# Up-projection block products: the order of modulation steps, one more PSUM bank, and an operand kept without its shift

## The chip, the cores and the metric

One core of a Trainium2 chip runs the whole program. The metric is the device time of one execution in microseconds (us). The kernel before took 2954.84 us (median of three runs, 2954.62 to 2957.98).

## The reference

A backbone of two layers over 1024 latent tokens and 256 context tokens, width 1024. Each layer has a token mixer and a ConvFFN, and each of the two reads its input through a modulated RMSNorm whose shift and scale come from conditioning vectors:

```python
ml = (silu(c) @ w_mod[i] + b_mod[i]).reshape(B, N_MOD, 1, D)    # six vectors for the latents
mc = (silu(c_ctx) @ w_mod[i] + b_mod[i]).reshape(N_MOD, D)      # six for the context
def modulate(x, shift, scale): return rms_norm(x) * (1.0 + scale) + shift
def conv_ffn(h, w_up, conv_w, conv_b, w_down):
    g, u = split(h @ w_up)                       # 2 x 2816 columns
    acc = conv_b + sum(shifted(g, j) * conv_w[j] for j in range(3))
    return (silu(acc) * u) @ w_down
```

The case is about `h @ w_up` in both layers. The context goes through layer 0's ConvFFN only.

## The kernel before

All tensors are held transposed: 128 channels on the partitions, tokens along the free dimension, in chunks 0 and 1 (512 latents each) and, in layer 0, chunk 2 (256 context tokens). A float32 product is made of three matmuls on a high and a low part of each operand (`mm3`, L72), so each operand is split: the high part is a rounded copy (ACT or POOL), the low part a subtraction (DVE).

**The up-projection** (class `Up`, L1615) makes 22 pairs f of a gate column block and an upper column block, each 128 wide. The first two, f = 0 and 1, are plain products (`plain`). From f = 2 on, gate and upper of both latent chunks are computed together as one 2x2 block product with seven products in place of eight (`PROD`): operands are sums of weight blocks (`s1` to `s4`, made by POOL, split by ACT and DVE) and sums of token blocks (`t1` to `t4`, class `Parts`, made once in the head). The products add up in three PSUM banks per f: x (products 1, 2), y (6, 7, 4) and z (5, 3). Between two products of one bank an engine reads the intermediate sum: `s1` (ACT, L1974) reads x between 1 and 2, `u2` (DVE, L1978) reads y between 6 and 7, `u3` (L1984) reads y after 7, `c22` (L1987) reads z between 5 and 3, `c11`, `c12` and `c21` finish gate and upper. In layer 0 the context's two plain products per f stand between them (`context`).

**Order of the work.** The order on PE, DVE, ACT and POOL is written out by hand in `head` (L1747: f = 0, 1, the token sums, and products 1 and 2 of f = 2) and `turn(f)` (L1848: products 6, 5, 7 of f, product 1 of the next f, product 3 of f, product 2 of the next, product 4 of f). SP, which issues the DMAs, is not in that hand-written order: its order is the planner's. In a turn ACT, DVE and POOL also do the short convolution (`conv`, `conv2`), silu and the product with the upper half (`mix`) of the f whose gate is finished; `store` writes the result row to DRAM. For f = 0 that stands in the head, for f = 1 in turn 2, ahead of `u2`. The result rows (`su`) are two buffers used in turn.

**Modulation vectors.** Layer 0's turns also make the modulation columns that come later. One step (`Up.mod`, L1739) takes one entry of `mods1` (53 are left when the turns start), loads 128x1024 weights into the single buffer `wm` (L1743) and reduces them on DVE (L325) against the conditioning vector: twice, for latents and context, in the first 21 entries, once in the other 32. For the scales (`n in (1, 4)`) a small POOL addition (L330) follows. A turn calls it three times: after `u2`, after product 7 (both ahead of `u3` and `c22` on DVE), and at the end.

**The operand.** For the ConvFFN's input `modulate_kept` (L255) overwrites the residual tile with the modulated operand, because the token sums need it: DVE or POOL scales it in place, ACT writes the high part and, for the operands that DVE scaled, in a second pass adds the shift in place (L272), DVE subtracts (L277).

**Weights.** The raw up-projection weights go through two buffers `raw` (L1633); f = 1's two blocks are split in the head, `raw[1,0]` at its start and `raw[1,1]` behind the chunk-1 gate product of f = 0.

Of the kernel before, what the change touches and what calls it, by code (L numbers as in the profile page):

```python
# [44 lines left out]
def backbone(tc, a):  # L45
# [209 lines left out]
    def modulate_kept(k, x, r, m, first, dst, pool=True):  # L255
# [6 lines left out]
        def scale():  # L262
            if even:
                V.scalar_tensor_tensor(out=x, in0=x, scalar=sc, in1=r, op0=ALU.mult, op1=ALU.mult)
            else:
                P.tensor_mul(x, x, r)
                P.tensor_scalar(out=x, in0=x, scalar1=sc, scalar2=sh, op0=ALU.mult, op1=ALU.add)
# [1323 lines left out]
    class Parts:  # L1591


        def __init__(self, up, j):
            self.up, self.j = up, j
            (self.b11, self.b12), (self.b21, self.b22) = [[xl[k][:, half_of(c)] for c in (0, 1)] for k in (j, j + 4)]
# [7 lines left out]
        def high(self, t, pair):  # L1604
            self.up.B[t, self.j] = pair
            S.copy(pair[0], self.src(t))
# [4 lines left out]
        def low(self, t):  # L1611
            hi, lo = self.up.B[t, self.j]
            V.tensor_sub(lo, self.src(t), f32(hi))

    class Up:  # L1615
# [3 lines left out]
        def __init__(self, l, sp, pairs, mods=()):  # L1619
# [3 lines left out]
            self.mods = list(mods)  # L1623
            self.raw, self.sums, self.A, self.B, self.bank, self.fs, self.spare = {}, {}, {}, {}, {}, {}, {}
            self.d_act = tc.dram_tile([NF, 128, T], F32, name=f"d_act{l}")
# [6 lines left out]
        def load(self, f, s):  # L1632
            self.raw[f, s] = wpool.tile([128, 1024], F32, name="raw", tag="raw", bufs=2)  # L1633
# [86 lines left out]
        def product(self, f, i):  # L1720
            w, b, z = self.PROD[i]
            first = i in (1, 6, 5)
# [16 lines left out]
        def mod(self, n=1):  # L1739
            for _ in range(n):  # L1740
                if self.mods:
                    j = self.mods.pop(0)
                    wm = self.sp.tile([128, D], F32, name="wm", tag="wm", bufs=1)  # L1743
                    mod_cols(*j, mod_load(*j[:3], wm), junk=self.tile("junk").bitcast(BF16))


        def head(self, w, b00, n1):  # L1747


            f0, f1 = F(self, 0), F(self, 1)  # L1750
            self.fs = {0: f0, 1: f1}
            ctx = 2 in self.chunks
# [3 lines left out]
            w1 = [self.halves(0)]  # L1756
            self.split_halves(self.raw[1, 0], w1[0])()
            self.load(2, 0)
# [12 lines left out]
            w1.append(self.halves(1))  # L1771
            self.split_halves(self.raw[1, 1], w1[1])()
            self.load(2, 1)
# [22 lines left out]
            t = [self.sp.tile([128, 1024], F32, name="wm", tag="wm", bufs=1)]  # L1796
            f0.temps = [t[0][:, :512], t[0][:, 512:]]
            for c in (0, 1):
                f0.conv(c)
                f0.conv2(c)  # L1800
                f0.silu(c)
            for c in (0, 1):
                f0.mix(c, V)
            if ctx:
                f0.conv(2)
                f0.conv2(2)
                f0.silu(2)
                f0.mix(2, V)
            f0.store()
# [11 lines left out]
            self.fs[2].s1()  # L1821
# [11 lines left out]
            self.product(2, 2)  # L1833
            self.fs[2].c11()
# [11 lines left out]
            self.spare["t"] = [x[6][:, 512:], x[7][:, :512], x[7][:, 512:]]  # L1846

        def turn(self, f):  # L1848
# [5 lines left out]
            if f == 2:  # L1854
                for c in (0, 1):
                    old.conv(c)
                    old.conv2(c)
                    old.silu(c)
            else:
# [7 lines left out]
            old.mix(1)  # L1867
            old.mix(0)
            if f == 2 and ctx:
                old.conv(2)  # L1870
                old.conv2(2)
                old.silu(2)
                old.mix(2)
            old.store()
# [10 lines left out]
            self.mod()  # L1885
# [7 lines left out]
            self.mod()  # L1893
# [6 lines left out]
            me.c22()  # L1900
            if not n:
# [41 lines left out]
    class F:  # L1943


        def __init__(self, up, f):
            self.up, self.f = up, f
            self.cw = [convw[:, up.l, i, f : f + 1] for i in range(4)]
            self.su, self.t, self.temps = row(1, name="su"), {}, None
# [4 lines left out]
        def open(self):  # L1954
            self.g = row(0, name="g")
# [24 lines left out]
        def c11(self):  # L1980
            S.copy(self.g_of(0), self.bank("x"))
# [28 lines left out]
        def mix(self, c, eng=P, u=None):  # L2010
            eng.tensor_mul(self.s_of(c), self.t[c], self.s_of(c) if u is None else u)  # L2011

# [111 lines left out]
    mods1 = [(0, 5, k, (0, 1)) for k in range(8)] + [(1, n, k, (0, 1) if n < 2 else (0,)) for n in range(6) for k in range(8)]  # L2124
    up = Up(0, sp, [("hi", "lo"), ("x", "y"), ("x", "y"), ("x", "z")], mods1)
# [79 lines left out]
    for i, *fs in (  # L2205
# [10 lines left out]
        if i > 12:  # L2216
            w0[i - 13] = wload(a["wup"][0, i - 13])
    o.product(15)
# [627 lines left out]
    for i in range(10, 15):  # L2846
        o.product(i)
        window(i, (n0, 2 * i - 20) if i < 14 else None, n1.add if i < 14 else last, lambda: up.spill(i - 9, 1))
        if i > 12:
            w0[i - 13] = wload(a["wup"][1, i - 13])  # L2850
    o.product(15)
# [7 lines left out]
    n1.split()  # L2859
    up.plain(w0[0], 0, range(6, 8), b00)  # L2860
    n1.total()
    w0[1] = w0[1]()
    up.load(1, 1)
    n1.root()
# [305 lines left out]
```

## Time and profile before

| | |
|---|---|
| median of the runs | 2954.84 us |
| profiled execution | 2955.65 us |
| its span (first to last instruction) | 2953.7 us |
| mean granted TensorE clock | 0.985 |
| PE matmul, PE weight load, DVE, ACT, POOL busy | 95, 79, 74, 43, 36% of the span |

PE is TensorE's matmul, DVE VectorE, ACT ScalarE, POOL GpSimd, SP the engine that issues DMAs ("SPq" its queue). Times in rows are us from the span's start. A granted clock of 1.00 is the upper level of TensorE's clock (2.4 GHz), 0.50 the lower (1.2 GHz). A row of the timeline gives start, duration, engine, line, operation, tiles (written <- read), shapes, and in brackets how long the engine stood before it and who released it.

Layer 0's up-projection takes from about 698 to 1342 us: turn 2 starts at 776.70 and turn 21, the last, at 1318.21. Layer 1's turn 2 starts at 2289.79, its turn 3 at 2317.75 and its turn 21 at 2668.63.

### The profile page before, as it was taken

Reading aid. Unit: us, or ns where it says so; the run is one execution under the profiler, and the core shown is the slowest. Engines: PE = TensorE matmul, PEld = TensorE weight load, DVE = VectorE, ACT = ScalarE, POOL = GpSimd, SP = SyncE. Lnnn points to the kernel's source line nnn. Section 1 sums busy time; section 2 is a strip of 40 time slices with the busy share of each in tenths; the row PEclk is TensorE's granted clock in tenths of the full one; section 3 lists DMA queues with packets and bytes.
Section 4 is the critical chain, followed back from the end, with each engine's and each line's share of the span. In section 5 each row is a group of like instructions: output and inputs, shape, how many; then the busy total and the mean of one; then the engine's idle time right before and its main releaser. Section 6 shows DMA issues by size and latency. Waiting matters only on the chain.

```text
span 2953.7 us, 40163 instructions
## 1 busy us (share of the span) xinstructions
PE 2798.1 (95%) x14654; PEld 2321.0 (79%) x14654; DVE 2179.0 (74%) x3639; ACT 1257.5 (43%) x2546; POOL 1062.0 (36%) x1069
## 2 busy tenths in 40 slices
PE   7988999999788999999999998999998999999997
PEld 3857888887677788788888777999876788887886
DVE  5688888777776766668776878888756556568766
ACT  5525888725422232332101444888744333333104
POOL 2142444752234444431101534444331444442112
PEclk9999999999899999999999999999999999999998
DMA  6144001372133333345221110000041222226311
GB/s 224 69 147 128 23 15 57 119 249 85 66 103 113 111 119 128 128 139 196 74 70 52 43 36 29 1 1 1 19 142 55 71 80 82 83 86 231 97 58 57
DMA packets 97229, 264.89 MB, mean 90 GB/s; under 512 B 11908, under 2 KB 21060, under 8 KB 96904
## 3 DMA queue, kind: packets, MB, share of 16 engines
q1 hardware_dynamic: 97032, 262.33, 26.6%
q8 instruction: 115, 1.88, 0.3%
q14 instruction: 82, 0.67, 0.1%
HBM read 212.53 MB, written 49.75 MB: 89 GB/s over the span
## 4 chain that ended last, share of the span: by engine, by line
PE 54%; DVE 10%; issue 4%; DMA 4%; ACT 3%; POOL 2%; DVEq 0%; ACTq 0%; POOLq 0%
PE d L72 18%; PE y L72 7%; PE x L72 6%; PE z L72 6%; PE p L72 4%; DMA wm<-in_wmod 3%; PE pv L1281 3%; PE b L72 3%; PE T L1268 2%; PE S L1201 1%; PE qk L72 1%; PE S L1203 1%; PE S L1202 1%; DVE x L325 1%; DVE wm L325 1%
## 5 line engine op out<-in xcount | busy, mean ns | idle before, releaser
L2072 DVE SCALAR_TENSOR_TENSOR x<-d,mod,x 128x512 f32<-128x512 f32 (+1 forms) x352 | 254.9, 734 | 95.9 <-PE d L72 94.7
L1250 POOL TENSOR_SCALAR p<-p,sm 128x1280 f32<-128x1280 f32 x128 | 171.2, 1338 | 288.3 <-DVE sm L1249 190.7
L1271 DVE TENSOR_TENSOR tl<-T,th 128x512 fp32r<-128x512 f32 x328 | 225.5, 687 | 46.8 <-ACT th L1270 42.0
L1281 PE MATMUL pv<-th,v 128*128 128x256 f32 x976 | 254.1, 309 | 1.4 <-ACT vo L1410 1.0
L1224 DVE TENSOR_REDUCE mx<-S 128x1 f32<-128x512 f32 (+1 forms) x400 | 233.8, 585 | 11.0 <-PE S L1203 3.8
L72 PE MATMUL d<-act,wh 128*128 128x512 f32 (+1 forms) x832 | 231.4, 364 | 0.0
L1270 ACT CAST th<-T 128x512 fp32r<-128x512 f32 x328 | 192.2, 586 | 84.2 <-PE T L1268 76.5
L2055 ACT CAST act<-act 128x512 fp32r<-128x512 f32 (+1 forms) x110 | 61.5, 577 | 385.5 <-PE d L72 230.5
L2011 POOL TENSOR_TENSOR su<-x,su 128x512 f32<-128x512 f32 (+1 forms) x83 | 132.3, 1598 | 255.9 <-ACT x L2008 167.2
L72 PE MATMUL x<-h,a1h 128*128 128x512 f32 x640 | 205.3, 402 | 18.0 <-ACT su L1974 15.6
L72 PE MATMUL b<-h,wh 128*128 128x512 f32 (+1 forms) x752 | 206.7, 362 | 5.7 <-DVE h L493 4.0
L1974 ACT COPY su<-x 128x512 f32<-128x512 f32 x40 | 23.5, 587 | 420.9 <-PE x L72 395.4
L1684 POOL TENSOR_TENSOR x<-raw 128x512 f32<-128x512 f32 x80 | 112.8, 1410 | 228.6 <-DMA raw<-in_wup 125.7
L1268 PE MATMUL T<-ident,p 128*128 128x128 f32 x1280 | 193.0, 272 | 1.5 <-POOL p L1250 1.5
L1268 PEld LDWEIGHTS T<-ident,p 128*128 128x128 f32 x1280 | 156.5, 140 | 34.9 <-POOL p L1250 3.2
L1281 PE MATMUL pv<-tl,v 128*128 128x256 f32 x656 | 177.4, 282 | 0.0
L1281 PEld LDWEIGHTS pv<-th,v 128*128 128x128 f32 x976 | 173.4, 189 | 2.4 <-ACT vo L1410 1.5
L72 PEld LDWEIGHTS d<-act,wh 128*128 128x128 f32 x832 | 149.0, 188 | 27.3
L72 PEld LDWEIGHTS b<-h,wh 128*128 128x128 f32 x752 | 133.1, 189 | 35.2 <-DVE h L493 5.4
L72 PEld LDWEIGHTS x<-h,a1h 128*128 128x128 f32 x640 | 122.9, 193 | 48.1 <-ACT su L1974 16.2
L72 PE MATMUL d<-act,wl 128*128 128x512 f32 (+1 forms) x416 | 151.5, 364 | 0.0
L325 DVE CUSTOM_DVE_ANT_0 wm<-wm,silc,bmod 128x1024 f32<-128x1024 f32 x72 | 108.6, 1508 | 53.0 <-DMA wm<-in_wmod 51.6
(501 smaller groups left out, 8188.7 us busy)
## 6 DMA issues: line engine op xcount, KB each, us to landing
raw<-in_wup SPq DMA_DIRECT2D x88, 512.0 KB, 3.4
wm<-in_wmod SPq DMA_DIRECT2D x72, 512.0 KB, 3.7
act<-d_act SPq DMA_DIRECT2D x88, 256.0 KB, 3.6
raw<-in_wdn SPq DMA_DIRECT2D x44, 512.0 KB, 4.3
raw<-in_wout SPq DMA_DIRECT2D x32, 512.0 KB, 3.4
d_act<-su SPq DMA_DIRECT2D x22, 640.0 KB, 3.5
d_act<-su SPq DMA_DIRECT2D x22, 512.0 KB, 2.8
raw<-in_win SPq DMA_DIRECT2D x20, 512.0 KB, 3.6
```

The lines of the kernel that those rows point to most:

```text
L72: PE.matmul(out, w, x, start=first and i == 0, stop=last and i == n - 1, skip_group_check=more)
L325: V.tensor_tensor_reduce(out=out, in0=wm, in1=silc[w], op0=ALU.mult, op1=ALU.add, scale=1.0, scalar=bmod[:, l, i : i + 1], accum_out=mod[l ...
L1224: V.reduce_max(mx[:, j : j + 1], s, axis=AX.X)
L1250: P.tensor_scalar(out=self.p, in0=self.p, scalar1=sm[:, 3:4], scalar2=1.0, op0=ALU.mult, op1=ALU.mult)
L1268: PE.transpose(tb[:, (2 * j + i) * 128 : (2 * j + i) * 128 + 128], rows[i].p[:, c : c + 128], ident)
L1270: S.copy(hi, tb)
L1271: V.tensor_sub(lo, tb, f32(hi))
L1281: PE.matmul(out[0], st, mv, start=(u + j == 0 and x == 0), stop=(u + j == n - 1 and x == len(ops) - 1))
L1684: eng.tensor_tensor(out=t, in0=self.src(f, x), in1=self.src(f, y), op=op)
L2011: eng.tensor_mul(self.s_of(c), self.t[c], self.s_of(c) if u is None else u)
L2055: S.copy(hi, f32(lo))
L2072: V.scalar_tensor_tensor(out=x, in0=b, scalar=mod[self.l, c // 2][:, 40 + d : 41 + d], in1=x, op0=ALU.mult, op1=ALU.add)
```

## The change

- `modulate_kept` no longer adds the shift to the kept tile. ACT makes the high part with the shift as bias, DVE the low part as (x + shift) - high. `Parts` adds the shift where a token sum needs it (t2: the shift of the lower block, t3: the difference `gap`, a new 128x4 tile).
- In the head, product 2 of f = 2 gets a bank "w" of its own. `s1` of f = 2 moves to the end of the head; `c11` of f = 2 becomes a DVE addition of bank w and the copied row, and moves into turn 2.
- The split of f = 1's weights (`second`) stands ahead of the head: `raw[1,1]` is loaded earlier, into the buffer `wm`, and split ahead of w0[1]'s low part; `raw[1,0]` is split behind `n1.root()`.
- Convolution, silu, mix and store of f = 0 and f = 1 become `rest()`: f = 1's stands behind `u2` in turn 2 (it stood ahead of it), f = 0's stays in the head in layer 0 and moves behind `u2` of turn 3 in layer 1, where f = 0 has rows of its own.
- `Up.mod` reduces the weights that the step before loaded, and then loads the next into the same single buffer. The second step of a turn moves behind `u3` and `c22`. Turn 2 has no first step. The entries of `mods1` are reordered: doubled and single ones alternate until the doubled ones are used up.

```diff
         def high():
-            if even:
-                S.activation(hi, x, AF.Identity, bias=sh)
-                S.activation(x, x, AF.Identity, bias=sh)
-            else:
-                S.copy(hi, x)
+            S.activation(hi, x, AF.Identity, bias=sh)
         def low():
-            V.tensor_sub(lo, x, f32(hi))
+            V.scalar_tensor_tensor(out=lo, in0=x, scalar=sh, in1=f32(hi), op0=ALU.add, op1=ALU.subtract)
...
-        def mod(self, n=1):
-            for _ in range(n):
-                if self.mods:
-                    j = self.mods.pop(0)
-                    wm = self.sp.tile([128, D], F32, name="wm", tag="wm", bufs=1)
-                    mod_cols(*j, mod_load(*j[:3], wm), junk=self.tile("junk").bitcast(BF16))
+        def mod(self):
+            if self.wm:
+                mod_cols(*self.wm.pop(), junk=self.tile("junk").bitcast(BF16))
+            if self.mods:
+                j = self.mods.pop(0)
+                self.wm.append((*j, mod_load(*j[:3], self.sp.tile([128, D], F32, name="wm", tag="wm", bufs=1))))
+        def second(self, s):
+            self.w1[s] = self.halves(s)
+            self.split_halves(self.raw[1, s], self.w1[s])()
+            self.load(2, s)
...
-            self.fs[2].s1()
             f1.upper(1, self.plain(w1[1], 1))
...
-            self.product(2, 2)
-            self.fs[2].c11()
+            self.product(2, 2, "w")
...
+            self.fs[2].s1()
+            self.mod()
...
             self.product(f, 6)
-            if f == 2:
-                for c in (0, 1):
-                    old.conv(c)
-                    old.conv2(c)
-                    old.silu(c)
-            else:
+            if f > 2:
                 old.c21()
...
             me.u2()
-            self.mod()
+            if f == 2:
+                old.rest()
+                me.c11(True)
+            else:
+                if f == 3 and not ctx:
+                    self.fs[0].rest()
+                self.mod()
...
-            self.mod()
             if n:
                 for s in ("s1", "s2", "s3"):
                     self.sum(n, s)
...
             me.u3()
             me.c22()
+            self.mod()
...
+    dbl, sgl = [[j for j in mods1[3:] if len(j[3]) == n] for n in (2, 1)]
+    mods1 = mods1[:3] + [x for p in zip(dbl, sgl) for x in p] + sgl[len(dbl) :]
...
+    up.load(1, 1)
     o.product(15)
...
     mod2(3)
+    up.second(1)
     up.plain(w0[0], 0, range(6, 8), b00)
     n1.total()
     w0[1] = w0[1]()
-    up.load(1, 1)
     n1.root()
+    up.second(0)
     up.head(w0, b00, n1)
```

## Rows read from the trace of the kernel before

**Rows 1.** The page, busy us, share of the span and instructions of each engine.
```profile
PE 2798.1 (95%) x14654; PEld 2321.0 (79%) x14654; DVE 2179.0 (74%) x3639; ACT 1257.5 (43%) x2546; POOL 1062.0 (36%) x1069
```

**Rows 2.** Stretches of layer 0: us, busy by engine, clock, DMA share, GB/s.
```profile
771.42:776.70 5.28, 5.28 (x12) 4.12 (x13) 3.70 (x6) 3.81 (x8) 0.00 (x0) 0.50 0.29 105
776.70:816.35 39.65, 29.02 (x134) 23.97 (x132) 25.96 (x34) 14.33 (x26) 13.55 (x13) 0.86 0.22 70
816.35:1026.82 210.47, 186.52 (x926) 153.13 (x924) 149.50 (x207) 57.94 (x98) 83.85 (x93) 0.98 0.33 110
1026.82:1292.97 266.15, 256.53 (x1322) 215.19 (x1320) 174.62 (x241) 83.15 (x140) 109.24 (x118) 1.00 0.37 122
1292.97:1318.21 25.24, 25.24 (x134) 21.53 (x133) 13.31 (x19) 8.28 (x14) 10.09 (x11) 1.00 0.41 141
```

**Rows 3.** The same view for layer 1: turn 2, and turns 3 to 20.
```profile
2289.79:2317.75 27.96, 22.00 (x86) 17.39 (x85) 15.74 (x21) 11.69 (x20) 9.80 (x10) 0.88 0.16 57
2317.75:2668.63 350.88, 350.88 (x1514) 284.22 (x1513) 211.99 (x270) 116.66 (x199) 171.22 (x163) 1.00 0.25 86
```

**Rows 4.** PE's waits in layer 0's turns 2 to 20: total us, times, longest.
```profile
PE z L72 <- DVE su L1987: 18.1, 14, 2.6
PE y L72 <- DVE x L1978: 12.6, 7, 8.3
PE x L72 <- DVE a1l L1673: 8.6, 10, 1.5
PE x L72 <- POOL a1h L1668: 2.4, 2, 1.2
```

**Rows 5.** PE's waits in layer 0's head, 698 to 776.7 us.
```profile
PE x L72 <- ACT su L1974: 6.3, 1, 6.3
PE p L72 <- DVE wl L111: 2.6, 2, 2.0
```

**Rows 6.** PE's waits in layer 1's head and turn 2, 2228 to 2318 us.
```profile
PE x L72 <- ACT su L1974: 9.2, 1, 9.2
PE y L72 <- DVE x L1978: 6.0, 1, 6.0
PE p L72 <- DVE h L277: 3.3, 5, 1.0
```

**Rows 7.** Timeline of ACT at the end of layer 0's head.
```profile
770.78 0.58 ACT L1974 COPY su<-x 128x512 f32<-128x512 f32 x1 [2.43 <-DMA d_act<-su]
```

**Rows 8.** Timeline of DVE in layer 0's turn 2: convolution, then u2.
```profile
780.49 0.74 DVE L2004 SCALAR_TENSOR_TENSOR x<-g,convw,x 128x512 f32<-128x512 f32 x1
...
788.60 0.48 DVE L2005 SCALAR_TENSOR_TENSOR x<-g,convw,x 128x256 f32<-128x256 f32 x1
...
790.14 0.68 DVE L1978 TENSOR_TENSOR x<-y,su 128x512 f32<-128x512 f32 x1
```

**Rows 9.** Timeline of SP's queue in layer 0's turn 3.
```profile
819.57 0.33 SPq L311 DMA_DIRECT2D wm<-in_wmod  x1
822.46 0.33 SPq L2014 DMA_DIRECT2D d_act<-su  x1
```

**Rows 10.** Timeline of DVE in layer 0's turn 3.
```profile
819.46 0.69 DVE L1993 TENSOR_TENSOR su<-y,su 128x512 f32<-128x512 f32 x1
...
823.09 1.42 DVE L325 CUSTOM_DVE_ANT_0 x<-wm,silc,bmod 128x1024 bf16<-128x1024 f32 x1 [1.21 <-DMA wm<-in_wmod]
...
825.77 1.22 DVE L1673 TENSOR_TENSOR a1l<-raw,a1h 128x1024 fp32r<-128x1024 f32 x1
830.04 2.27 DVE L325 CUSTOM_DVE_ANT_0 x<-wm,silc,bmod 128x1024 bf16<-128x1024 f32 x1 [3.05 <-DMA wm<-in_wmod]
...
834.29 0.69 DVE L1987 TENSOR_TENSOR su<-z,su 128x512 f32<-128x512 f32 x1
```

**Rows 11.** Timeline of DVE and POOL in layer 0's head, token sums.
```profile
752.53 1.67 POOL L1684 TENSOR_TENSOR x<-raw 128x512 f32<-128x512 f32 x1 [52.42 <-DVE t L1613]
753.08 1.67 DVE L1600 TENSOR_TENSOR x<-x 128x512 f32<-128x512 f32 x1
```

More of the change, by code (lines that the diff above doesn't have):

```diff
@@ L1605, in high @@
             self.up.B[t, self.j] = pair
-            S.copy(pair[0], self.src(t))
+            if t in self.shift:
+                S.activation(pair[0], self.src(t), AF.Identity, bias=self.shift[t])
+            else:
+                S.copy(pair[0], self.src(t))
         def src(self, t):
@@ L1612, in low @@
             hi, lo = self.up.B[t, self.j]
-            V.tensor_sub(lo, self.src(t), f32(hi))
+            if t in self.shift:
+                V.scalar_tensor_tensor(out=lo, in0=self.src(t), scalar=self.shift[t], in1=f32(hi), op0=ALU.add, op1=ALU.subtract)
+            else:
+                V.tensor_sub(lo, self.src(t), f32(hi))
     class Up:
@@ L1718, in operand, with product @@
             return H[c][j + 4 * k]
-        def product(self, f, i):
+        def product(self, f, i, own=None):
             w, b, z = self.PROD[i]
-            first = i in (1, 6, 5)
+            first = i in (1, 6, 5) or own is not None
+            z = own or z
             if first:
@@ L1795, in head @@
                 p.low(1)
[L1796 to L1809 removed]
+            if ctx:
+                t = self.sp.tile([128, 1024], F32, name="wm", tag="wm", bufs=1)
+                f0.temps = [t[:, :512], t[:, 512:]]
+                f0.rest()
             f1.gate(1, self.plain(w1[0], 1))
@@ L1866, in turn @@
                     down.act_load(e)
[L1867 to L1874, printed above, removed]
+            if f > 2:
+                old.mix(1)
+                old.mix(0)
+                old.store()
             self.alow(f, 1)
@@ L1978, in u2, with c11 @@
             V.tensor_add(self.u, self.bank("y"), self.s_of(0))
-        def c11(self):
-            S.copy(self.g_of(0), self.bank("x"))
+        def c11(self, apart=False):
+            if apart:
+                V.tensor_add(self.g_of(0), self.bank("w"), self.s_of(0))
+            else:
+                S.copy(self.g_of(0), self.bank("x"))
         def u3(self):
@@ L2011, in mix, with rest @@
             eng.tensor_mul(self.s_of(c), self.t[c], self.s_of(c) if u is None else u)
+        def rest(self):
+            for c in (0, 1):
+                self.conv(c)
+                self.conv2(c)
+            for c in (0, 1):
+                self.silu(c)
+                self.mix(c, V)
+            if 2 in self.up.chunks:
+                self.conv(2)
+                self.conv2(2)
+                self.silu(2)
+                self.mix(2, V)
+            self.store()
         def store(self):
@@ L2850, in backbone @@
             w0[i - 13] = wload(a["wup"][1, i - 13])
+    up.load(1, 1)
     o.product(15)
@@ L2859, in backbone @@
     n1.split()
+    up.second(1)
     up.plain(w0[0], 0, range(6, 8), b00)
@@ L2862, in backbone @@
     w0[1] = w0[1]()
-    up.load(1, 1)
     n1.root()
+    up.second(0)
     up.head(w0, b00, n1)
```

32 lines of the change are left out of this document (17 added, 15 removed).

## The prediction

> **What bounds the kernel now.** The page's busy times come first [rows 1]: TensorE (PE) is busy for 95% of the span and the next engine, VectorE (DVE), for 74%. So a change pays only where PE stands still, or where the granted clock is down. The stretches of the two up-projections come next. In layer 0 the five stretches of [rows 2] run from the end of the head to the last turn: turn 20, with no gap at all, takes 25.24 us, which is the floor of a layer-0 turn; turn 2 takes 39.65, turns 3 to 9 take 210.47 (30.07 each), turns 10 to 19 take 266.15 (26.6 each). In layer 1 [rows 3] turns 3 to 20 take 350.88, or 19.49 each, and PE is busy for all of it: nothing is to be won there. Seven products in 19.49 make 2.79 us a product. Turn 2 of layer 1 takes 27.96.
>
> So 61.9 us over the floor lie in layer 0's turns 2 to 20 (14.4 in turn 2, 47.5 after it), 8.5 in layer 1's turn 2, and some in the heads. The list of waits says who ended PE's gaps. In layer 0's turns [rows 4]: 18.1 us for `c22` (L1987), which must read bank z before product 3 adds to it; 12.6 for `u2` (L1978), 8.3 of it at once in turn 2; 8.6 for a1's low part; 2.4 for its high part on POOL. In layer 0's head [rows 5]: 6.3 for the copy `s1` (L1974), which must read bank x before product 2 adds to it, and 2.6 for a low part (L111). In layer 1 up to turn 2 [rows 6]: 9.2 for `s1`, 6.0 for `u2`, 3.3 for the low parts of the modulated operand (L277). A gap also brings the clock down: after layer 0's 6.3 us gap twelve matmuls took 5.28 us at a granted 0.50, the lower of the two levels [rows 2], where 2.79 is the product at the upper one: 2.5 us.
>
> **The change part by part.** The sum is made against the profiled execution, 2955.65 us (span 2953.7), which is 0.8 above the median 2954.84.
>
> **Own bank for the head's second product.** Product 2 no longer adds to bank x, so it doesn't wait for `s1`. Layer 0: the gap of 6.3, its refill (0.3) and the 2.5 at half clock go, 9.1 together. Layer 1: 9.2, 0.3 and 2.1 go, 11.6. The price is `c11` as a DVE addition out of PSUM instead of an ACT copy, 0.69 us like L1987 [rows 10], in turn 2. Also `s1` moves behind the last splits, so ACT no longer stands for the store of f0's row there, 2.43 us [rows 7].
>
> **f1's weights split early.** The split of `raw[1,1]` now stands ahead of w0[1]'s low part on DVE: two more 128x512 subtractions of 0.69. In layer 0 PE already waits for that low part (part of the 2.6 in [rows 5]): +1.3, and I add 1.0 for a lower clock behind the longer gap (bounds 0 and the 2.5 seen). In layer 1 PE shows no wait there, and I cost it at nothing: earlier PE work covers it, and without the cover it is the same 1.3.
>
> **Shift out of the operand.** One ACT pass per operand goes; the low part becomes a three-operand DVE op of the kind that takes 0.74 us [rows 8] against 0.69. This can give back at most the 3.3 of [rows 6], at least 0; I take 3.0, since DVE then has only two ops per operand and ACT one. Layer 0 shows no such wait, so nothing. The later operands with a bias add under 0.1 us each and lie beside PE work.
>
> **f1's convolution behind `u2`.** In turn 2, DVE did the convolution [rows 8], a2's low part and then `u2` at 790.14, while PE stood 8.3. Now `u2` comes first. `u2` ended at 790.8; without the chain of 8.5 us ahead of it (780.49 to 789.0) and with ACT 2.9 earlier (the 2.43 and a copy) it ends near 779.4. PE starts turn 2 6.8 earlier (the head's sum, below), at 769.9, and reaches product 7 two products later, at 775.5: a wait of 3.9 stays (bounds 0 and the old 8.3). What is queued behind the moved work is a1's low part, and product 1 of the next f waits for that: four ops of 0.75, two mixes of 0.69, the third chunk's three of 0.5, `c11` 0.69 and about 1 us for ACT's silu, then 1.22 for the low part [rows 8, 10]: 8.5 us after `u2`, where PE wants it 3.3 after (one product and two matmuls). So a new wait of 5.2. Bounds: 0, if it fills DVE's idle time, and 9. With 0.6 of refill and 1.5 of clock, turn 2 becomes 25.24+3.9+5.2+2.1 = 36.4: it gives 3.2. Layer 1 lacks the third chunk, so 6.5 stand in place of 8.5 and 3.2 in place of 5.2; f0's convolution has left its head too, so ACT and DVE come sooner and I take 2.0 for the wait at product 7, between 0 and 3.9: 19.49+2.0+3.2+1.5 = 26.2, which gives 1.8; f0's convolution, moved to turn 3 behind `u2`, costs 1.0 there in the same way (bounds 0 and 3).
>
> In the heads, then: layer 0 gives 9.1-2.3 = 6.8, layer 1 11.6+3.0 = 14.6.
>
> One row speaks against the moved convolution: a DVE subtraction of two SBUF tiles took 1.67 us beside a POOL addition [rows 11], where ops of its size take 0.69 [rows 10]. POOL's a1 high part now falls beside the moved convolution. The Trainium skill (SBUF — State Buffer, "Who interferes with whom") has it that a DVE op with both inputs in SBUF contends with GpSimd's reads; by that rule each turn 2 would be about 1 us longer, and the total about 2 us more than mine, by the row's difference. I leave it inside the range.
>
> **Modulation weights.** The load one step ahead gives nothing by itself: the buffer is single, and the load is already issued at 819.57 [rows 9], where the last reduction ends and `c21` starts [rows 10]. What pays is the place of the second step. Today DVE waits 3.05 us for its load until 830.04, reduces twice, and only then runs `u3` and, at 834.29, `c22` [rows 10]; now `u3` and `c22` stand ahead of it, and the 18.1 us for `c22` go. The first step stays between `u2` and a1's low part. There the alternation of double and single reductions helps: a pair of steps (last of one turn, first of the next) has three reductions instead of four, 1.3 less (half of the 2.68 from 823.09 to 825.77), against waits of 1.5 for a1's low part. I keep 0.6 per turn in turns 3 to 10. In turns 11 to 16 a doubled scale (n=1) or an n=4 puts its POOL addition ahead of a1's high part, the 2.4 us of [rows 4]: 2.2 per turn. Turns 17 to 20: 0.3. With 3.0 for clock: 4.8+13.2+1.2+3.0 = 22.2 of the 47.5 remain, and 25.3 go. Bounds: all 47.5, or 11 (rival 2).
>
> **Sum:** 6.8+3.2+25.3 in layer 0, 14.6+1.8-1.0 in layer 1: 50.7. 2955.65-50.7-0.8 is about 2904.
>
> **The rivals.** (1) *Clean turns.* The alternation takes the first step off the path, and turns 3 to 20 all run at 25.24. For: turn 20. Against: the DMA wait of 1.21 at 823.09 [rows 10] stays. Another 22 go: 2882.
>
> (2) *The first step takes the waits over.* Doubled reductions now reach into turn 16 instead of 9. If the a1 wait stays at 1.8 in 14 turns with 7 more for POOL and 4 of clock, 36 of the 47.5 remain, so 11.5 go instead of 25.3, and turn 2's chain is 4 longer in each layer: 2926.
>
> (3) *Slower: the load lands behind the store.* SP's order isn't written by hand. Today the load for the first step (819.57) precedes the store of the old row, which waits for POOL until 822.46 [rows 9]. If the new place of the load puts it behind that store, it is issued 6.1 us into a turn (turn 3 starts at 816.35), lands 3.5 later, and with 2.7 or 1.3 for the reductions and 1.2 for the low part a1 is ready at 13.5 or 12.2 where PE wants it at 8.8: 4.0 plus refill in 18 turns is 77, and 22 of clock: 99 against 47.5. With the 25 won elsewhere (6.8+3.2+15.4): 2980. It decides from about 4.0 us lost per turn ((47.5+25)/18). The Trainium skill (DMA: Bandwidth & Descriptors, "Anatomy of one DMA") says that DMA engines don't wait on semaphores and the issuing sequencer does, before dispatch; by that a load behind a waiting store is held with it, as this rival assumes. Against: the planner put the load first already, and it now stands earlier in the program.
>
> (4) *Nothing moves.* The waits for `s1` and `u2` pass to a1 whole and the one for `c22` to the first step: about 2950.
>
> **How the numbers follow.** Forecast 0.55, rival 1 0.13, rival 2 0.21, rival 3 0.06, rival 4 0.05. The range, 2880 to 2930, takes in the forecast with its bounds and rivals 1 and 2. A measurement of this kernel tells about 0.2% (5.9 us) from no change; so faster 0.89, same 0.05 (rival 4), slower 0.06 (rival 3).
>
> **What would show it.** Right: no PE wait for L1974 or L1987; layer 1's product 2 directly behind its predecessor; in both turns 2 a gap before a1's low part in place of the one before product 7; layer-0 turns near 26 before turn 11. Wrong: SP rows with the `wm` load behind the store, a1 gaps of over 2 us in turns 3 to 10, or a head gap at L111 of well over 4 us.

## The result, and the profile after

The changed kernel takes 2917.30 us (median of 4, 2915.77 to 2921.26) against 2954.73 for the kernel before in the same comparison: a ratio of 0.9877, 95% interval 0.9859 to 0.9894, or 37.4 us less. The forecast was 2904, 50.7 less, in a range of 2880 to 2930.

On the page PE stays the busiest engine, as in [rows 1], in a span that went from 2953.7 to 2916.3:

```profile
PE 2793.6 (96%) x14654; PEld 2319.8 (80%) x14654; DVE 2201.5 (75%) x3646; ACT 1242.3 (43%) x2520; POOL 1075.8 (37%) x1066
```

Stretches of the changed kernel, to be read beside [rows 2, 3] (columns as there): layer 0's head, counted from the last matmul of the sum of squares (`ss`) ahead of it to the start of turn 2; turn 2; turns 3 to 10, 11 to 16 and 17 to 20; then layer 1's head in the same way, its turn 2, turn 3, and turns 4 to 20.

```profile
705.30:769.73 64.43, 61.09 (x314) 51.67 (x314) 44.46 (x64) 27.21 (x47) 5.22 (x7) 0.97 0.06 20
769.73:809.55 39.82, 30.54 (x134) 24.96 (x132) 31.50 (x41) 18.39 (x34) 13.87 (x11) 0.83 0.27 94
809.55:1022.71 213.16, 205.58 (x1057) 170.82 (x1056) 161.91 (x216) 65.51 (x110) 91.47 (x88) 1.00 0.38 124
1022.71:1191.37 168.66, 158.62 (x793) 129.84 (x792) 119.70 (x162) 50.80 (x86) 80.75 (x87) 0.98 0.35 118
1191.37:1292.40 101.03, 101.03 (x529) 86.04 (x528) 67.12 (x92) 33.10 (x56) 44.88 (x47) 1.00 0.40 133
2204.72:2250.40 45.68, 45.07 (x195) 35.99 (x193) 36.04 (x50) 20.79 (x35) 4.67 (x5) 1.00 0.07 23
2250.40:2281.18 30.78, 24.27 (x85) 18.86 (x84) 24.10 (x32) 15.20 (x26) 12.43 (x9) 0.83 0.19 69
2281.18:2303.01 21.83, 19.74 (x85) 15.72 (x84) 17.17 (x21) 9.23 (x16) 10.24 (x10) 1.00 0.27 97
2303.01:2633.72 330.71, 330.71 (x1430) 268.56 (x1428) 199.06 (x255) 109.72 (x188) 161.36 (x153) 1.00 0.25 86
```

The two heads of the kernel before, in the same view and between the same marks:

```profile
704.58:776.70 72.12, 63.75 (x314) 53.55 (x314) 48.39 (x70) 36.43 (x63) 6.52 (x8) 0.91 0.14 46
2228.14:2289.79 61.65, 48.85 (x195) 37.34 (x193) 44.29 (x62) 33.12 (x54) 6.41 (x6) 0.92 0.12 43
```

| stretch | before | after | measured | forecast |
|---|---|---|---|---|
| layer 0's head | 72.12 | 64.43 | -7.7 | -6.8 |
| its turn 2 | 39.65 | 39.82 | +0.2 | -3.2 |
| turns 3 to 20 | 501.86 | 482.85 | -19.0 | -25.3 |
| layer 1's head | 61.65 | 45.68 | -16.0 | -14.6 |
| its turn 2 | 27.96 | 30.78 | +2.8 | -1.8 |
| its turn 3 | 19.49 | 21.83 | +2.3 | +1.0 |

These make 37.4; the stretches between them cancel to within 0.1 (from +2.4 between the layers to -2.5 behind layer 1's turns). PE's waits of the changed kernel in layer 0's turns, beside [rows 4]:

```profile
PE x L72 <- DVE a1l L1683: 13.8, 15, 4.9
PE y L72 <- DVE x L1979: 7.6, 8, 4.3
PE x L72 <- POOL a1h L1678: 5.0, 3, 2.1
```

`c22` and `s1` are gone from the list, the waits for a1 and `u2` (L1979) are what is left. In layer 0's head the `s1` of [rows 5] is gone and the low part (L111) has grown to 3.3, as forecast. In layer 1, beside [rows 6]:

```profile
PE x L72 <- DVE a1l L1683: 5.6, 2, 3.5
PE y L72 <- DVE x L1979: 3.0, 1, 3.0
PE p L72 <- DVE h L273: 0.6, 2, 0.4
```

### The profile page after: what moved, and what is told of

It is laid out like the page before. It is cut to its first block, busy times and chain, and to the rows that moved or that the text cites. A ratio compares the mean times of both kernels' runs of the same rounds, so it can differ in the third digit from the quotient of the medians.

```text
span 2916.3 us, 40138 instructions
## 1 busy us (share of the span) xinstructions
PE 2793.6 (96%) x14654; PEld 2319.8 (80%) x14654; DVE 2201.5 (75%) x3646; ACT 1242.3 (43%) x2520; POOL 1075.8 (37%) x1066
## 4 chain that ended last, share of the span: by engine, by line
PE 56%; DVE 11%; ACT 3%; issue 3%; DMA 2%; POOL 1%; DVEq 0%; SPq 0%; ACTq 0%; POOLq 0%
PE d L72 18%; PE y L72 7%; PE x L72 6%; PE z L72 5%; PE p L72 5%; PE pv L1277 3%; PE b L72 3%; DMA wm<-in_wmod 2%; PE T L1264 2%; PE S L1197 1%; PE qk L72 1%; PE S L1199 1%; PE S L1198 1%; DVE x L2008 1%; DVE x L321 1%
## 5 line engine op out<-in xcount | busy, mean ns | idle before, releaser
L1220 DVE TENSOR_REDUCE mx<-S 128x1 f32<-128x512 f32 (+1 forms) x400 | 234.0, 585 | 10.9 <-PE S L1199 3.7
L1694 POOL TENSOR_TENSOR x<-raw 128x512 f32<-128x512 f32 x80 | 119.5, 1493 | 237.2 <-DMA raw<-in_wup 136.1
L2015 POOL TENSOR_TENSOR su<-x,su 128x512 f32<-128x512 f32 x78 | 125.9, 1616 | 218.3 <-ACT x L2012 123.7
L72 PE MATMUL x<-h,a1l 128*128 128x512 f32 x312 | 128.1, 411 | 19.4 <-DVE a1l L1683 19.4
```

The source lines that it names most:

```text
L72: PE.matmul(out, w, x, start=first and i == 0, stop=last and i == n - 1, skip_group_check=more)
L1220: V.reduce_max(mx[:, j : j + 1], s, axis=AX.X)
L1694: eng.tensor_tensor(out=t, in0=self.src(f, x), in1=self.src(f, y), op=op)
```

## The experiments

Each was measured beside the kernel before, and each ratio is to that. The same code in the same place differs from run to run: layer 0 from its `ss` to turn 3 took 103.2 to 105.9 us in six kernels with the same code there. A total within 5.9 us of another, the prediction's 0.2%, is called no difference, and parts are read from the waits and stretches.

| kernel | median us | ratio, 95% interval |
|---|---|---|
| shared_bank | 2915.65 | 0.9871, 0.9854 to 0.9888 |
| conv_in_head | 2917.64 | 0.9876, 0.9860 to 0.9892 |
| shift_back | 2919.39 | 0.9881, 0.9866 to 0.9895 |
| three_back | 2927.11 | 0.9905, 0.9891 to 0.9918 |
| rest_first | 2918.48 | 0.9874, 0.9860 to 0.9888 |
| rest_later | 2914.70 | 0.9863, 0.9849 to 0.9878 |
| second_back | 2938.89 | 0.9947, 0.9934 to 0.9959 |
| no_alternation | 2909.56 | 0.9847, 0.9833 to 0.9860 |
| step_after_low | 2902.17 | 0.9822, 0.9807 to 0.9837 |
| alt_after_low | 2903.53 | 0.9826, 0.9812 to 0.9839 |
| low_before_all | 2901.30 | 0.9821, 0.9807 to 0.9834 |
| third_earlier | 2883.72 | 0.9759, 0.9745 to 0.9773 |

### The heads: the bank, the convolution, the shift

**shared_bank**

```diff
-            self.product(2, 2, "w")
+            self.product(2, 2)
+            self.fs[2].c11()
...
-            self.fs[2].s1()
             self.mod()
...
-                me.c11(True)
```

with `s1` ahead of `f1.upper(1, ...)` again.

> Edit: the head's second product adds to bank x again, with s1 ahead of it and the ACT copy c11 behind it in the head, as before the change; all else is the changed kernel (2917.3 us). Theory (the bank was the whole of the heads' gain): PE waits for s1 again, about 6 us and a slow product of 2.5 in layer 0, about 9 and 2 in layer 1, less 0.7 twice for the DVE addition that turn 2 loses: 2934 to 2938. Rival (s1 would come soon enough now, since f0's convolution has left layer 1's head and ACT and DVE have one pass less per operand there): the waits for s1 stay under 3 us in each layer and the whole is 2919 to 2924.

Both were wrong: nothing was lost. Layer 0's head and turn 2, then layer 1's, in the view of the stretches:

```profile
704.26:775.88 71.62, 62.80 (x313) 52.86 (x314) 48.28 (x70) 31.84 (x55) 6.48 (x8) 0.95 0.12 39
775.88:809.84 33.96, 27.34 (x134) 22.55 (x133) 25.75 (x35) 14.46 (x26) 9.47 (x10) 0.90 0.20 66
2202.34:2249.59 47.25, 45.34 (x195) 35.94 (x193) 37.58 (x51) 22.33 (x38) 6.07 (x6) 1.00 0.07 23
2249.59:2278.11 28.52, 22.01 (x86) 17.20 (x85) 22.63 (x28) 14.04 (x24) 10.41 (x9) 0.88 0.22 74
```

Layer 0's head takes 71.62, as before the change, and PE waits 5.5 for `s1`. But turn 2 then takes 33.96 in place of 39.82, and turn 3 starts at 809.84 in place of 809.55. The bank brings PE to turn 2 earlier by 7.2 us, and turn 2 hands 5.9 of it back: its end is set by DVE (PE's last wait in it is for a1's low part in both kernels). What is left, 1.3, is inside the spread above. In layer 1 the wait for `s1` is 1.3, not 9.2.

**conv_in_head** (f0's convolution back in layer 1's head, own bank kept)

```diff
-            if ctx:
+            if True:
                 t = self.sp.tile([128, 1024], F32, name="wm", tag="wm", bufs=1)
...
-                if f == 3 and not ctx:
-                    self.fs[0].rest()
```

> Edit: in layer 1, f0's convolution, silu, mixes and store stand in the head again instead of behind u2 in turn 3; own bank and all else as in the changed kernel (2917.3 us). Layer 0 is not touched. Theory (layer 1's gain of some 13.6 us before its turn 2 came from this work leaving the head, since the run with the shared bank kept that gain): the waits for s1 or for the splits behind the convolution return, and layer 1's turn 4 starts 5 to 10 us later against the end of layer 0 (1010.6 us after layer 0's turn 21 in the changed kernel); the whole 2922 to 2927. Rival (the gain is that of the operands without the shift, or the own bank makes up for the convolution): layer 1's turn 4 stays within 3 us, less the 2.3 us that turn 3 loses, and the whole is 2913 to 2919.

The rival held: 2917.64. Layer 1's head took 48.88 us (45.68 with the convolution out of it); turn 2 was 28.46 and turn 3 19.45, which gave back more than that (30.78 and 21.83).

**shift_back**

```diff
+                S.activation(hi, x, AF.Identity, bias=sh)
+                S.activation(x, x, AF.Identity, bias=sh)
...
-            V.scalar_tensor_tensor(out=lo, in0=x, scalar=sh, in1=f32(hi), op0=ALU.add, op1=ALU.subtract)
+            V.tensor_sub(lo, x, f32(hi))
...
-            self.shift = {2: sh[:, j + 4 : j + 5], 3: up.gap[:, j : j + 1]}
+            self.shift = {}
```

> Edit: the shift is added to the operand in place again (two ACT passes, or POOL's with the shift) and the later operands take no bias; all else as in the changed kernel (2917.3 us). Theory (the shift is a term of at most 3 us, as the prediction had it): PE's waits for the low parts of the modulated operand in layer 1 return to about 3.3 us from 0.6, and the whole is 2918 to 2921. Rival (the ACT passes that went were what s1 and the splits stood behind, so that most of layer 1's 13.6 us is due to them): layer 1's turn 2 starts 8 to 12 us later and the whole is 2924 to 2930.

As the theory had it: the wait for the low parts is 2.5 us again, layer 1's head 49.60, 3.9 longer; turn 2 is 2.5 shorter and turn 3 1.5 longer (23.29), so that 2.8 stay up to turn 4. The total, 2919.39, is too near the changed kernel's to show the part.

**three_back** puts shared_bank, conv_in_head and rest_first (below) together, with f0's rows among the ordinary ones: `F(self, 0)` in place of `F(self, 0, 2 not in self.chunks)`.

> Edit: three parts undone together that cost nothing when undone singly: the head's second product adds to bank x again with s1 ahead of it and c11 behind it; f0's convolution is back in layer 1's head with f0's rows among the ordinary ones; f1's convolution stands ahead of a2's low part and u2 again. The modulation steps, the early split and the shift stay as in the changed kernel (2917.3 us). Theory (own bank and convolution out of the way are two ways round the same chain of DVE and ACT, so that either alone gives the gain and only both undone lose it): layer 1's wait for s1 returns with 7 to 9 us and its turn 4 starts 6 to 9 us later against the end of layer 0 (1010.6 us in the changed kernel, 1019.0 before the change); layer 0's turn 3 starts at 812 to 815 us in place of 809.6; the whole 2926 to 2932. Rival (the heads' gain is that of the early split and the shorter operand chain): layer 1's turn 4 within 3 us of the changed kernel's, layer 0's turn 3 before 811.5, whole 2914 to 2921.

The total came out where the theory had it, 9.8 us over the changed kernel, but in part by luck (below). Stretches of layer 0's head, its turn 2, and layer 1's head:

```profile
706.41:778.90 72.49, 63.72 (x315) 53.50 (x315) 48.88 (x70) 31.82 (x55) 6.62 (x9) 0.93 0.12 39
778.90:813.46 34.56, 27.73 (x133) 23.20 (x132) 22.95 (x33) 14.41 (x25) 7.78 (x10) 0.90 0.20 65
2206.76:2263.93 57.17, 48.30 (x194) 37.71 (x193) 43.93 (x61) 27.44 (x44) 6.53 (x7) 0.91 0.11 37
```

and layer 1's wait for `s1`:

```profile
PE x L72 <- ACT su L1973: 8.4, 1, 8.4
```

So in layer 1 either part alone, the bank or the moved convolution, removes most of the 9.2 of [rows 6]: its head takes 47.25 with the convolution out of it, 48.88 with the bank, 57.17 with neither (f0's own rows stayed in the first two). Layer 0's turn 3 starts at 813.46, inside the theory's bounds. What the theory had wrong is that layer 1 keeps the loss: its turns 2 and 3 take 44.70 us here (25.21 and 19.49) against 52.61, so turn 4 is only 1.8 later against the start of layer 0's turn 21, where 6 to 9 were expected. In the profiled executions the difference is 9.0: 2.8 in layer 0 up to turn 3, 3.6 in layer 1 up to turn 4, and 3.4 from there to the end (turns 4 to 20 take 331.39, the rest 285.28, against 330.71 and 282.58), which the theory had nothing for (the last section has more on it); the stretches ahead and between take 0.8 off. And three_back is still far from the kernel before: layer 0 from `ss` to turn 3 takes 107.05 against 111.77, layer 1 from its own `ss` to turn 4 101.87 against 109.10. The early split of f1's weights, the missing first step of turn 2 and f1's mixes, which `rest()` does on DVE where turn 2 had them on POOL, were not undone by themselves, and how they share in this is open.

### Turn 2: what its end hangs on

**rest_first**

```diff
             if f > 2:
                 old.c21()
+            else:
+                old.rest()
...
             if f == 2:
-                old.rest()
                 me.c11(True)
```

> Edit: in turn 2 of both layers f1's convolution, silu and mixes stand ahead of a2's low part and u2 again; all else is the changed kernel (2917.3 us). Theory (the move only exchanges the wait for u2 with the one for a1's low part, as layer 0's turn 2 of 39.82 us against 39.65 before says): PE waits 7 to 9 us for u2 and under 1 us for a1's low part, one stretch at the low clock stays, each turn 2 is within 2 us of what it is now and the whole 2914 to 2921. Rival (the move does pay, and something else has made turn 2 longer): each turn 2 is 3 to 6 us longer and the whole 2923 to 2929.

The total stayed, but not quite by the theory's road: in layer 0's turn 2 PE waits once, longer than the theory had it, and not at all for a1; the turn takes 39.40 (39.82 in the changed kernel). Its only group of waits:

```profile
PE y L72 <- DVE x L1980: 12.0, 1, 12.0
```

One gap of 12.0 with one slow stretch behind it (PE busy 27.37) costs as much as two of 4.3 and 4.9 with two (30.54): the convolution's place decides where PE stands, not when the turn ends.

**rest_later** (f1's convolution behind a1's parts, ahead of `u3` and `c22`)

```diff
             if f == 2:
-                old.rest()
-                me.c11(True)
+                pass
...
                 self.alow(n, 0)
+            if f == 2:
+                old.rest()
+                me.c11(True)
+            elif f == 3 and not ctx:
+                self.fs[0].rest()
```

> Edit: in turn 2 of both layers f1's convolution (and in layer 1's turn 3 f0's) stands behind a1's high and low parts, still ahead of u3 and c22; alternation and all else as in the changed kernel (2917.3 us). Theory (the waits for a1's low part, 4.9 and 3.5 us, go, and the next wait is c22's, behind the convolution; product 1 is done by then): turn 2 of layer 0 takes 35 to 37 us in place of 39.8, that of layer 1 28 to 29.5 in place of 30.8, and the whole is 2910 to 2914. Rival 1 (the low clock goes with the gap too): 31 and 27, whole 2904 to 2908. Rival 2 (the wait moves to c22 whole): both turns within 1 us of now, whole 2916 to 2919.

The wait for a1 goes, and `c22` takes over only 1.8 of it in layer 0: turn 2 is 33.98 there, but turn 3 grew from 26.07 to 27.18. Layer 1's turn 2 is 29.36, and 5.6 us of waits for `c22` in its turns 2 and 3 replace those for a1. The total, 2914.70, is just above the theory's bounds and no difference by itself.

### The loop: the modulation steps

**second_back**

```diff
                 self.context(f, 1)
+            if f > 2:
+                self.mod()
...
             me.c22()
-            self.mod()
+            if f == 2:
+                self.mod()
```

> Edit: from turn 3 on, the second modulation step stands ahead of u3 and c22 again; all else is the changed kernel (2917.3 us). Theory (the loop's gain comes from c22 no longer standing behind the second step): PE's waits for c22 return, some 2.3 us in each of the seven turns with a doubled second step (4, 6, ... 16), 10 to 18 us in all; layer 0's turns 3 to 20 take 493 to 501 us in place of 482.9, and the whole 2927 to 2935. Rival (DVE's amount of work per turn sets the pace and the order only names another wait): turns 3 to 20 stay within 3 us of 482.9, the waits for a1's low part shrink by what c22's grow, and the whole is 2914 to 2920.

The theory's direction, and more of it than foreseen: turns 3 to 20 take 505.12 us, 22.3 more than in the changed kernel, and the whole is 21.6 slower. The largest group of waits in them is `c22`'s:

```profile
PE z L72 <- DVE su L1994: 20.9, 10, 3.5
```

Undone alone, the second step's place takes back 21.6 of the change's 37.4 us, more than any other part undone here.

**no_alternation**

```diff
-    mods1 = mods1[:3] + [x for p in zip(dbl, sgl) for x in p] + sgl[len(dbl) :]
+    mods1 = mods1[:3] + dbl + sgl
```

> Edit: the modulation steps in the order of before (all doubled ones first); all else is the changed kernel (2917.3 us). Theory (a late first step costs more than in proportion, so spreading the doubled ones pays): turns 3 to 9 take about 29 us each, turns 11 to 20 about 25.7, turns 3 to 20 together 490 to 494 in place of 482.9; the whole 2925 to 2928. Rival (each doubled step costs the same wherever it stands): turns 3 to 9 take about 27.5 to 28, what they lose comes back in turns 11 to 16, and the whole is 2914 to 2920.

The theory was wrong in sign: 7.7 us less than the changed kernel. The rival had turns 3 to 9 right (27.9 on average), but more than what they lose comes back behind them. Turns 3 to 10 and 11 to 20 in the view of the stretches, against 213.16 and 269.69 (168.66 and 101.03) with the alternation:

```profile
809.47:1030.08 220.61, 207.70 (x1058) 171.82 (x1056) 172.56 (x232) 66.07 (x112) 100.14 (x104) 0.99 0.36 120
1030.08:1284.63 254.55, 253.53 (x1321) 214.68 (x1320) 175.95 (x237) 83.51 (x141) 111.43 (x118) 1.00 0.39 131
```

The alternation gains 7.5 us up to turn 10 and loses 15.1 behind it, since it spreads the doubled steps into turns where single ones cost next to nothing: 254.55 is within 2.2 of ten clean turns of 25.24.

The timeline of DVE, SP and PE in the changed kernel at the start of turn 5 shows the chain. The last step of turn 4 runs on into turn 5 (which begins at 861.74), the next load is issued when it ends (865.49), the first step waits for that, and a1's low part stands behind it; PE waits 1.51 there.

```profile
863.23 0.69 DVE L1702 TENSOR_TENSOR s4l<-x,s4h 128x512 fp32r<-128x512 f32 x1 [1.09 <-ACT s4h L1698]
...
864.17 1.28 DVE L321 CUSTOM_DVE_ANT_0 wm<-wm,silc,bmod 128x1024 f32<-128x1024 f32 x1
...
865.49 0.33 SPq L307 DMA_DIRECT2D wm<-in_wmod  x1
...
868.77 1.64 DVE L321 CUSTOM_DVE_ANT_0 x<-wm,silc,bmod 128x1024 bf16<-128x1024 f32 x1 [0.98 <-DMA wm<-in_wmod]
...
871.67 1.22 DVE L1683 TENSOR_TENSOR a1l<-raw,a1h 128x1024 fp32r<-128x1024 f32 x1
...
872.94 0.50 PE L72 MATMUL x<-h,a1l 128*128 128x512 f32 x1 [1.51 <-DVE a1l L1683]
```

Two edits take the first step out of this chain. **step_after_low** (steps in the old order) and **alt_after_low** (alternated) move the first step behind a1:

```diff
             if n:
                 self.ahigh(n, 0, P)
                 self.alow(n, 0)
+            if f > 2:
+                self.mod()
```

in place of the `self.mod()` ahead of them.

> Edit: modulation steps in the old order (as in the run without the alternation, 2909.6 us), and from turn 3 on the first step of a turn stands behind a1's high and low parts instead of ahead of them; the second stays behind c22. Theory (in every turn product 1 waits for the step that stands ahead of a1's low part, and DVE has nothing to do for 0.6 to 1 us before that step, since it waits for its load): the waits for a1's low and high parts, 8.5 and 3.9 us in turns 3 to 20, fall below 3, turns 3 to 7 take 25.3 to 26 us in place of 27.4, turns 8 to 10 under 27, and the whole is 2892 to 2898. Rival (DVE's later ops then come later by as much: c22 or the first product of the next turn waits): turns 3 to 7 stay above 26.7 us and the whole is 2904 to 2912.

> Edit: the changed kernel (2917.3 us, alternation kept) with the first step of a turn behind a1's high and low parts, ahead of u3 and c22. Theory (the alternation lost because POOL's additions and the doubled first step stood ahead of a1; behind a1 they are out of the way, and spreading the doubled steps over turns 3 to 16 leaves DVE enough time in each turn, where turns 4 to 9 of the run in the old order waited 1.5 to 2.3 us for u2): no wait for a1 in turns 3 to 20, turns 3 to 16 of 25.3 to 26.2 us, turns 3 to 20 together 457 to 466 us against 470.3 in the old order, the whole 2889 to 2898. Rival (the alternation costs by itself, whatever stands ahead of a1, as each odd turn ends with the step that delays u2): odd turns over 27 us up to turn 15, the whole 2900 to 2908.

2902.17 lies between theory and rival, 2903.53 inside the bounds of alt_after_low's rival, though no odd turn up to 15 is over 27 us (25.25 to 26.63). In both the waits for a1 went as the theories had it, and what came in their place is nearer to step_after_low's rival: DVE's later work was late. Every wait for a1 in turns 3 to 20 is gone, POOL's too, but `u2`'s grow, from 1.0 in no_alternation and 3.2 in the changed kernel. Step_after_low's only group of waits in turns 3 to 20, then alt_after_low's:

```profile
PE y L72 <- DVE x L1980: 11.7, 7, 2.3
```

```profile
PE y L72 <- DVE x L1980: 11.2, 12, 1.6
```

With the step out of a1's way the order of the steps makes no difference (470.25 and 468.72 us for turns 3 to 20).

**low_before_all** adds rest_later's and conv_in_head's edits to alt_after_low.

> Edit: as the kernel with the first step behind a1 (alternation kept), and in turn 2 of both layers f1's convolution behind a1 as well, and in layer 1 f0's convolution in the head. Theory (these parts add up: layer 0's turn 3 came 3.7 us earlier with the convolution behind a1 and turn 3 itself took 1.1 longer; layer 1's turn 4 came 2.9 earlier with f0's convolution in the head): 3 to 6 us less than the kernel with the first step behind a1 alone, 2885 to 2893. Rival (turn 2's lateness is carried into turn 3, and layer 1's gains don't add): within 2 us of the kernel with the first step behind a1 alone.

The rival's size: 2.2 us less, no difference. Layer 0 reaches turn 3 3.6 us earlier than in alt_after_low, but layer 1 reaches turn 4 2.0 later, both counted from `ss`.

**third_earlier** moves the last step of a turn as well, and puts f1's convolution ahead of a1 again in layer 1:

```diff
+            if ctx:
+                self.mod()
             if n:
                 self.high(n, "s4")
                 self.low(n, "s4")
             if ctx:
                 me.mix(2, V, self.bank[f, "c", 1])
-                self.mod()
```

> Edit: the kernel of the run before (first step behind a1, alternation kept, f1's convolution behind a1 in layer 0, f0's in layer 1's head; 2901.3 us) with two things changed: the last step of a layer-0 turn stands ahead of s4's low part, where DVE waits 1.1 us for ACT, instead of behind it and the third chunk's mix; and in layer 1's turn 2 f1's convolution stands ahead of a1 again. Theory (what is left in turns 3 to 16 is u2, 10.9 us in 13 waits of at most 1.6, late because the last step reaches into the next turn; filling the 1.1 us gap takes most of each wait away): turns 3 to 16 take 25.3 to 25.9 us in place of 25.2 to 27.0 (mean 26.2), turns 3 to 20 together 458 to 464 us in place of 468.2; the whole 2889 to 2895. Rival (the last step waits there for its own load, or s4's low part and the mix are then late by as much): turns 5 to 16 stay at a mean over 26.0 us, the whole 2897 to 2902.

Better than the theory: 2883.72. Layer 0's turns 3 to 20 in one stretch, against 468.20 in low_before_all:

```profile
804.57:1259.12 454.55, 454.55 (x2378) 387.55 (x2377) 339.48 (x469) 149.72 (x254) 204.06 (x222) 1.00 0.40 131
```

PE is busy throughout, 25.25 us a turn: the clean turns of rival 1. In the DVE timeline around the start of turn 8 (930.82), s4's low part no longer waits for ACT, and `u2` (L1981) ends at 935.93, ahead of product 7, which starts at 936.39:

```profile
931.38 1.28 DVE L321 CUSTOM_DVE_ANT_0 wm<-wm,silc,bmod 128x1024 f32<-128x1024 f32 x1
...
932.59 0.69 DVE L1702 TENSOR_TENSOR s4l<-x,s4h 128x512 fp32r<-128x512 f32 x1
...
935.25 0.68 DVE L1981 TENSOR_TENSOR x<-y,su 128x512 f32<-128x512 f32 x1
```

Moving a step into a 1.1 us gap of DVE was worth 13.65 us in the loop. It beats both kernels: 70 us less than before the change, 34 less than after it. Of its gain over low_before_all, 17.6, some 4 lie outside the loop: 1.6 in layer 0's turn 2 and 1.0 in layer 1's; the rest was not located.

## Why the prediction was right, and where it was not

The forecast gave 13.3 us too much: 6.3 in layer 0's turns 3 to 20, and 9.3 in the two turns 2 and layer 1's turn 3, less 2.3 that the heads gave beyond it.

**The second step's place: right.** `c22` no longer waits, and putting the step back costs 22.3 us of turns 3 to 20.

**The rest of the loop: two steps wrong.** The first is "There the alternation of double and single reductions helps". Without the alternation the loop gains 26.7 (501.86 to 475.16) in place of 19.0. The prediction counted reductions per pair of steps; it knew that the load is issued only when the last reduction ends, but did not follow this on: a late step delays two.

The second is "With 3.0 for clock". The loop left 28.5 us over the floor where 22.2 were forecast: 11.2 in turns 3 to 10 against 4.8, 17.2 in turns 11 to 16 against 13.2, and 0.1 against 1.2 after them. But the waits in them, for which the sum had 19.2 (4.8+13.2+1.2), are only 17.0 in the changed kernel:

```profile
PE x L72 <- DVE a1l L1683: 8.8, 14, 1.5
PE x L72 <- POOL a1h L1678: 5.0, 3, 2.1
PE y L72 <- DVE x L1979: 3.2, 7, 1.1
```

Nearly all of the rest is that PE's matmuls took longer: it was busy for 205.58 and 158.62 us in turns 3 to 10 and 11 to 16, and clean turns make 201.92 and 151.44. That is 10.9 where the sum had 3.0. Turns 11 and 13 have 4.6 of it, at a granted clock of 0.94:

```profile
1022.71:1052.83 30.12, 27.48 (x134) 22.35 (x132) 19.34 (x28) 9.20 (x16) 12.06 (x12) 0.94 0.33 110
1079.26:1110.17 30.91, 27.56 (x134) 22.38 (x132) 19.61 (x30) 9.19 (x16) 11.49 (x14) 0.94 0.32 107
```

The other 6.3 lie in the turns with a granted 1.00; over the 19 waits there this is 0.33 each, about the 0.3 of refill that the prediction put behind a gap in the heads and left out here. Its 2.2 per turn for turns 11 to 16 was too high as a wait (9.9 in all against 13.2): the 2.4 of [rows 4] beside which it stands is the sum of two waits, of at most 1.2.

**The own bank: the size right where it was looked for, its worth wrong.** The heads were forecast at -6.8 and -14.6 and measured -7.7 and -16.0. But the sum took the terms as independent. Undone alone the bank costs nothing (shared_bank), since turn 2 ends when DVE is done; in layer 1 the convolution's move does the same service. That layer 1's head came out near the forecast, with 11.6 of it put down to the bank, is luck in this sense. Only with three parts undone is something lost, 6.4 us up to layer 0's turn 3 and layer 1's turn 4. The 2.1 for the lower clock in layer 1, for which the prediction names no row, is right: before the change the product behind the 9.2 us gap took 4.92 us (2284.87 to 2289.79) in place of 2.79.

**Turn 2: the size of the waits right, its end wrong.** The prediction's sign, a gap before a1's low part in place of the one before product 7, came half: both gaps are there. `u2` was to cost 3.9 and a1 5.2 in layer 0; they cost 4.3 and 4.9. The second agrees by chance. The step that failed is the chain behind `u2`, "8.5 us after `u2`": `u2` ended at 779.64, close to the 779.4 of the forecast, but a1's low part at 790.76, 11.1 later. PE's wait for it did not grow because PE was late as well: behind the first gap it ran at the lower level, and product 7 took 5.26 us (779.79 to 785.05) in place of 2.79. Behind the second gap it was slow again; both stretches in the view of the windows:

```profile
778.30:785.80 7.50, 6.01 (x14) 4.47 (x14) 7.43 (x8) 2.05 (x4) 4.91 (x4) 0.54 0.20 70
788.90:795.50 6.60, 4.69 (x12) 3.72 (x13) 5.64 (x9) 0.02 (x1) 0.00 (x0) 0.50 0.24 99
```

The granted clock is 0.54 and 0.50. From a1's low part to the end of the turn PE took 18.7 us; a turn of 25.24 less three products of 2.79 and half a microsecond is 16.4. So the clock cost 2.4 on the path in place of 1.5, and the chain 2.6 more: that is the 3.4 by which the turn was missed, to half a microsecond. In the terms of the sum it is the refill and the clock that were too small: the two waits make 9.2 against 9.1, but PE is busy 5.3 longer than in a clean turn (30.54 against 25.24), where 2.1 were put. In layer 1 `u2` cost 3.0 in place of 2.0, a1 3.5 in place of 3.2 behind a chain of 8.7 (2258.98 to 2267.63) in place of 6.5, and PE was busy 4.8 longer (24.27 against 19.49) in place of 1.5: most of the 4.6 by which that turn was missed.

What lengthened the chain stands in the timeline of DVE and POOL in layer 0's turn 2:

```profile
775.18 4.77 POOL L1678 TENSOR_SCALAR a1h<-raw 128x1024 fp32r<-128x1024 f32 x1 [3.42 <-DMA raw<-in_wup]
...
782.46 1.40 POOL L1694 TENSOR_TENSOR x<-raw 128x512 f32<-128x512 f32 x1 [2.52 <-DMA raw<-in_wup]
782.64 3.46 DVE L2015 TENSOR_TENSOR su<-x,su 128x512 f32<-128x512 f32 x2
783.94 1.61 POOL L1694 TENSOR_TENSOR x<-x,raw 128x512 f32<-128x512 f32 x1
785.51 1.71 POOL L1694 TENSOR_TENSOR x<-raw 128x512 f32<-128x512 f32 x1
786.02 1.48 DVE L2008 SCALAR_TENSOR_TENSOR x<-g,convw,x 128x256 f32<-128x256 f32 x1
```

Beside POOL's sums two mixes took 1.73 each in place of 0.69, and one 128x256 step 1.48 in place of 0.48: 3.1 us. The prediction had about 1 for this, as a sentence beside the sum. The Trainium skill (SBUF — State Buffer, "Who interferes with whom") says that a DVE instruction with two SBUF inputs contends with a GpSimd one that reads SBUF; these rows agree. No run took the contention away alone. That these mixes stand on DVE at all is part of the change, though its list does not say so: before, turn 2 did f1's mixes on POOL.

**The shift: about right,** 3.0 forecast, 3.9 measured at layer 1's turn 2 and 2.8 at its turn 4, in stretches; the total doesn't show it.

**Rival 2 came half.** The wait for a1's low part is now the largest in the loop, but 0.6 us on average over its 14 times where rival 2 had 1.8; POOL's high part added 5.0 of its 7, and the clock and the refill more than its 4.

**Rival 3 was not there.** SP still issues the load ahead of the store, as in [rows 9], and that as soon as the last reduction ends:

```profile
811.60 0.33 SPq L307 DMA_DIRECT2D wm<-in_wmod  x1
814.50 0.33 SPq L2033 DMA_DIRECT2D d_act<-su  x1
```

A second buffer, which would make the load truly one step ahead, was not tried.

## What to carry to other kernels

Gains read from separate waits add up only if the next wait is not set by the same engine: before crediting a part, ask what the stretch ends with if PE arrives earlier. Price a gap by its wait and by the slower matmuls behind it: in the loop 17.0 us of waits came with 10.9 us of those. Where a prefetch has a single buffer, a late step delays the step after it too, so here the place of each step in the turn counted for more than the number of reductions in it. Look for the short idle spots of the engine that is nearly the bound, and put movable work there: that brought the turns to their floor, which spreading the work alone did not. Whether the old order of the steps would get there too was not run.

## What the runs showed of the hardware that was not expected

POOL's 128x1024 cast a1h took 4.77 us (775.18, above) beside an unbroken run of DVE operations, which kept their usual length (a2's low part 1.22, `u2` 0.68); in layer 1 it took 3.77 (2255.51), beside such a run as well. The same cast takes 1.05 at 870.49 in no_alternation, where DVE stood for its load until 870.95. At 782.64 it was DVE that was stretched. Spans on POOL are rough, so the 4.77 is a reading, not a price.

In layer 1's PE-bound turns a turn takes 19.45 us in the changed kernel and 19.49 before, and the stretch behind layer 1's turns is 2.5 us shorter. Of the runs only three_back, which has f0's rows among the ordinary ones, shows 19.49 and the longer stretch again. So it goes with the tiles of f0's rows, but no run changed these alone, and the cause stays open.
